# LayerNorm of the convolution branch, put inside the last four projection groups of a hybrid Conformer/gMLP layer

## Chip, cores and metric

The kernel runs on one core of one Trainium2 chip. The metric is the time of one execution on the device in microseconds (us); lower is better.

## The reference, cut to what matters

One layer over a sequence of 2048 positions with 1024 channels. A combined projection of the normalised input gives eight parts. Branch A, with which the change deals, is: GLU, a causal depthwise convolution of width 31, a LayerNorm over the channels, SiLU, a product with a SiLU gate, and a projection `w_conv_out`. Branch B is a gated mixing of positions that ends in a projection `w_sgu_out`.

```python
p = h @ w_in[l]
a = val * sigmoid(glu)
y = depthwise_causal_conv(a, conv_w) + conv_b          # width 31
y = silu(layernorm(y, ln_g, ln_b)) * silu(z)           # over the 1024 channels
y_a = y @ w_conv_out
merged = sigmoid(gA) * y_a + sigmoid(gB) * y_b
x = x + gate * (merged @ w_o[l])                       # then a final RMSNorm
```

All of it is float32. The kernel splits each operand of the large products into a high and a low part and adds three products of parts.

## The kernel before, in words

**Passes and halves.** The sequence is worked in two passes (`s` = 0 and 1) of 1024 positions, and each pass in two halves (`h`) of 512. Channels lie on the 128 partitions, in eight tiles (`j`).

**Groups.** The combined projection is made of 28 groups per pass (`quad`, L646), each a Strassen-like form of a 2 by 2 block product: seven products of 12 matmuls of 128x512 (`prod`). A group's order on TensorE is: its first product, the seventh product of the group before it (`pending`), then its second to sixth product. After the second to the sixth product an eviction follows on ScalarE or VectorE. Eight times come the three groups `glu(j)`, `uz(j)`, `spilled(j)`; the last four groups make the SiLU gate `z`, which is written to DRAM (`d_sz`) and read again later. Weight pieces are prepared four pieces ahead (`AHEAD`): a high half on ScalarE (L87) and a low half on GpSimd or VectorE (L88).

**The order of the work.** The code is traced from top to bottom, and every instruction gets a priority number in that order. The framework's planner then simulates the program and writes a fixed order of instructions for each engine: where several are ready, the one with the lowest number goes first. Each engine on the chip runs its list in that order and waits where an input is late. A background list `bg` holds small units of work; `run_bg(n)` (L319) traces the next n of them with 800 (`LATER`) added to their numbers, so that they fill gaps. It is called seven times with n = 2 in a group (six times where no `pending` is there), and with n = 4 after each product block of the two projections that follow.

**The convolution** (L693) is such background work: per tile `j` one ScalarE step and 30 VectorE steps of 128x1024 (L704), which sum in `wide()`, a pair of PSUM banks with one buffer, then `add_y` (L715), which adds the tile into `s1`. Those of the last tile run into the first of the last four groups.

**The LayerNorm** stands after the groups, on the list of the projection of branch B (`std_pairs(yb, ...)`): `mean(h)` sums `s1` over the channels with a matmul with ones (L166); `centre(h, j)` subtracts it (L835), squares (L839, L842) and adds (L843) into `rsq`; `ln_rstd(h)` makes the sums of columns with four matmuls of one column (L144), a root and a reciprocal (L137, L138), and spreads the result over the partitions (L154, L161, L852). `mean` and `ln_rstd` take PSUM banks from the six that the products use too. `conv_out(h, j)` (L854) then applies scale, SiLU and `z`, and splits the result into `ya[h][j]`. In the first pass 18 units for the token statistics of the next pass stand ahead of these on the list. `std_pairs(ya, ...)`, the projection of branch A, needs the `ya` tiles of a half as its inputs. Each of the two projections has 16 product blocks of 24 matmuls.

**Buffers.** `s1` and `rsq` share a single buffer of the tag `row`. The products and the norm share `t512` (six buffers). `yb` and `ya` come from 28 buffers `hs`, which the operands of the groups hold until the groups have used them. Loads of `z`, of the gates and of `x` for the statistics share three buffers `ld`.

Of the kernel before, what the change touches and what calls it, by code (L numbers as in the profile page):

```python
# [10 lines left out]
AF = mybir.ActivationFunctionType  # L11
ALU = mybir.AluOpType
# [4 lines left out]
D = 1024  # L17
SEQ = 2048
KT = D // P
KH = KT // 2  # L20
T = 512
S = 2 * T
NS = SEQ // S
NC = T // P
# [11 lines left out]
LATER = 800  # L36
# [4 lines left out]
def hybrid_layer(  # L41
    ctx: ExitStack, tc, x, xt, wada, wgate, vecs, rows, wst, w_in, w_v, w_a, w_b, w_o, out
):
    nc = tc.nc
# [9 lines left out]
    def bank():  # L54
        return ps.tile([P, 512], F32, tag="ps", name="bank", bufs=6)

    def wide():
        return ps.tile([P, S], F32, tag="cv", name="cv", bufs=1)

    def t512(name="t512", dtype=F32):  # L60
        return tmp.tile([P, T], dtype, tag="t512", name=name, bufs=6)
# [11 lines left out]
    def row(name):  # L73
        return tmp.tile([P, S], F32, tag="row", name=name, bufs=1)

    def load(src, name="ld"):
        t = tmp.tile([P, T], F32, tag="ld", name=name, bufs=3)
        nc.sync.dma_start(out=t, in_=src)
        return t
# [18 lines left out]
    def col(base, j):  # L98
# [4 lines left out]
    ones = const.tile([P, P], F32, name="ones")  # L103
# [3 lines left out]
        out=ident, in_=ones, pattern=[[1, P]], compare_op=ALU.is_ge, fill=0.0,  # L107
# [3 lines left out]
        out=ident, in_=ident, pattern=[[-1, P]], compare_op=ALU.is_ge, fill=0.0,  # L111
# [22 lines left out]
    def rstd_cols(src, n):  # L134

        c = sm.tile([P, 8], F32, tag="cols", name="cols")[:, :n]
        nc.scalar.activation(c, src, AF.Sqrt, bias=eps_t, scale=1.0 / D)  # L137
        nc.vector.reciprocal(out=c, in_=c)  # L138
        return c

    def col_sums(val, pt, first, n):

        for c in range(n):
            nc.tensor.matmul(  # L144
                pt[:, first + c : first + c + 1], val[:, c * P : (c + 1) * P], one,
                start=True, stop=True,
            )

    def spread(cols, pt=None):

        diag = t512("diag")
        nc.vector.tensor_tensor(  # L154
            out=diag.rearrange("p (c t) -> p c t", t=P),
            in0=ident.rearrange("p (c t) -> p c t", c=1).broadcast_to([P, NC, P]),
            in1=cols.rearrange("p (c t) -> p c t", t=1).broadcast_to([P, NC, P]),
            op=ALU.mult,
        )
        pt = bank() if pt is None else pt  # L160
        nc.tensor.matmul(pt, ones, diag, start=True, stop=True)  # L161
        return pt

    def sums(val):
        pt = bank()
        nc.tensor.matmul(pt, ones, val, start=True, stop=True)  # L166
        return pt
# [149 lines left out]
    bg = []  # L317

    def run_bg(n):  # L319
        tc.cur_priority += LATER  # L320
        for _ in range(min(n, len(bg))):
            bg.pop(0)()
        tc.cur_priority -= LATER


    def load_xn(s, h, xn):
# [135 lines left out]
    with tc.manual_schedule(engines=MANUAL):  # L462
        nc.vector.tensor_copy(out=base[:, :, 0], in_=vec[:, V_BSH : V_BSH + KT])
        nc.vector.scalar_tensor_tensor(
            out=base[:, :, 1], in0=vec[:, V_BSC : V_BSC + KT], scalar=1.0,
            in1=vec[:, V_GPRE : V_GPRE + KT], op0=ALU.add, op1=ALU.mult,
# [8 lines left out]
        for k in range(KT):  # L475
            v = xn[k][:, :T]
            if k == 0:
                nc.scalar.activation(acc, v, AF.Square)
            else:
                q = t512("q")  # L480
                nc.scalar.activation(q, v, AF.Square)
                nc.vector.tensor_tensor(out=acc, in0=acc, in1=q, op=ALU.add)
        pc = bank()
# [30 lines left out]
        for k in range(KT):  # L514
            t, v = A[0][k], xn[k][:, :T]
            nc.vector.tensor_tensor(
                out=t[:, 1], in0=v, in1=t[:, 0].bitcast(F32), op=ALU.subtract
# [17 lines left out]
            if k + 1 < KT:  # L535
                for u in range(2 * NC):
                    c, n = u // 2, u % 2
# [3 lines left out]
                for u in range(2 * NC):  # L541
                    c, n = u // 2, u % 2
# [6 lines left out]
        for u in range(2 * NC):  # L549
            c, n = u // 2, u % 2  # L550
# [6 lines left out]
            if u == 5:  # L557
                pc = bank()
# [13 lines left out]
        out=ws3, in_=ws3, pattern=[[0, KT], [1, P]], compare_op=ALU.is_ge, fill=0.0,  # L572
# [17 lines left out]
    for s in range(NS):  # L590
# [55 lines left out]
        def quad(c11, c12, c22, c21, in_psum):  # L646

            tt = nc.vector.tensor_tensor

            def snap(pt):  # L650
                t = t512("snap")
                nc.scalar.activation(t, pt, AF.Copy)  # L652
                return t

            a, d = bank(), bank()
            prod(a, [take()], A11)
            nc.scalar.activation(d, a, AF.Copy)  # L657
            run_bg(2)
            if pending:
                pending.pop()()  # L660
                run_bg(2)
            prod(a, [take()], A12, start=False)
            c11(a)
            run_bg(2)
            c = bank()
            prod(c, [take()], S1)
            p5 = snap(c)
            run_bg(2)
            prod(d, [take()], S2, start=False)
            p16 = snap(d)  # L670
            run_bg(2)
            if beside:
                beside.pop()()
            prod(c, [take()], S4, start=False)
            dst = c if in_psum else p16
            tt(out=dst, in0=c, in1=p16, op=ALU.subtract)
            c12(dst)
            run_bg(2)
            prod(d, [take()], S3, start=False)
            tt(out=p5, in0=p5, in1=d, op=ALU.subtract)  # L680
            c22(p5)
            run_bg(2)

            def end():
                prod(d, [take()], A22, start=False)
                c21(d)

            pending.append(end)

        s1 = []  # L690
        y = [None] * KT
# [90 lines left out]
        def spilled(func, d0, d1):  # L782


            def from_psum(dst):
                def fin(pt):
                    t = t512("sp")
                    nc.scalar.activation(t, pt, func)
                    nc.scalar.dma_start(out=dst, in_=t)

                return fin

            def from_sbuf(dst):
                def fin(p):
                    nc.scalar.activation(p, p, func)
                    nc.scalar.dma_start(out=dst, in_=p)

                return fin

            quad(  # L800
                from_psum(d0[0]), from_sbuf(d1[0]), from_sbuf(d1[1]), from_psum(d0[1]), False
            )

        for j in range(KT):
            glu(j)
            uz(j)
            spilled(AF.Sigmoid, d_sa[j], d_sbg[j])
        for i in range(KH):
            spilled(AF.Silu, d_sz[2 * i], d_sz[2 * i + 1])
        pending.pop()()  # L810
        run_bg(len(bg))


        yb = [[], []]
        for h in range(2):
            for j in range(KT):
                t = hs("yb")
                nc.sync.dma_start(
                    out=t.bitcast(F32).rearrange("p s c -> p (s c)"), in_=d_yb[j][h]
                )  # L820
                yb[h].append(t)

        pmu = []
        rsq = []
        ya = [[None] * KT, [None] * KT]

        def mean(h):
            pmu.append(sums(s1[0][:, h * T : (h + 1) * T]))

        def centre(h, j):  # L830
            hh = slice(h * T, (h + 1) * T)
            if not rsq:
                rsq.append(row("rsq"))
            v = y[j][:, hh]
            nc.vector.scalar_tensor_tensor(  # L835
                out=v, in0=pmu[h], scalar=-1.0 / D, in1=v, op0=ALU.mult, op1=ALU.add
            )
            if j == 0:
                nc.scalar.activation(rsq[0][:, hh], v, AF.Square)  # L839
            else:  # L840
                q = t512("q")
                nc.scalar.activation(q, v, AF.Square)  # L842
                nc.vector.tensor_tensor(  # L843
                    out=rsq[0][:, hh], in0=rsq[0][:, hh], in1=q, op=ALU.add
                )

        def ln_rstd(h):
            hh = slice(h * T, (h + 1) * T)
            pc = bank()
            col_sums(rsq[0][:, hh], pc, 0, NC)  # L850
            pr = spread(rstd_cols(pc[:, :NC], NC), pc)
            nc.scalar.activation(rsq[0][:, hh], pr, AF.Copy)  # L852

        def conv_out(h, j):  # L854
            hh = slice(h * T, (h + 1) * T)
            v = y[j][:, hh]
            z = load(d_sz[j][h], "zl")
            nc.vector.tensor_tensor(out=v, in0=v, in1=rsq[0][:, hh], op=ALU.mult)
            nc.scalar.activation(v, v, AF.Silu, bias=col(V_LNB, j), scale=col(V_LNG, j))
            nc.vector.tensor_tensor(out=v, in0=v, in1=z, op=ALU.mult)  # L860
            ya[h][j] = hs("ya")
            split(ya[h][j], v)

        if not last:
            rs_next = []
            for h in range(2):
                ss, sq = token_stats(s + 1, h)
                bg.extend(sq)
                bg.append(lambda ss=ss, h=h: rs_next.append(token_rstd(ss, f"rsn{h}")))
        for h in range(2):  # L870
            bg.append(lambda h=h: mean(h))
        for h in range(2):
            bg.extend(lambda h=h, j=j: centre(h, j) for j in range(KT))
            bg.append(lambda h=h: ln_rstd(h))
        for h in range(2):
            bg.extend(lambda h=h, j=j: conv_out(h, j) for j in range(KT))

        def std_pairs(rhs, done):

# [52 lines left out]
        if s == 0:  # L932
            for n in range(2):
# [3 lines left out]
                    out=gate[:, ns], in0=sums(acc[0][:, ns]), in1=bg_row, op=ALU.add  # L937
# [193 lines left out]
```

## Time and profile before

| | us |
|---|---|
| median of 3 runs | 1946.08 (1945.91 to 1950.67) |
| the profiled execution | 1949.32 |
| its span, first to last instruction | 1947.6 |

| engine | busy us in the span |
|---|---|
| TensorE | 1859.1 (95%) |
| VectorE | 1290.7 (66%) |
| ScalarE | 867.6 (45%) |
| GpSimd | 859.9 (44%) |

The mean granted clock of TensorE is 0.98 of 2.4 GHz. A busy share is an average over stages with different limits; matmuls overlap, so a busy TensorE is not one at its peak. What ended a wait is inferred from semaphores.

### The profile page before, as it was taken

To read this page: it belongs to the slowest core of one execution; us is meant where nothing else is said; L and a number is where in the kernel's file an instruction comes from. 1 tells how busy PE (TensorE), PEld (TensorE's weight loads), DVE (VectorE), ACT (ScalarE), POOL (GpSimd) and SP (SyncE) were. 2 spreads that over 40 slices of the span, in tenths; PEclk is the share of its full clock that TensorE was granted. 3 is DMA by queue.
4 is the path that set the end of the run, shared out by engine and by line. 5 is a ranking of instruction groups with operands and counts; after the bars stand their busy time and mean duration, and the time that the engine had idled before them with its cause. 6 is when DMAs were issued, how large, how long until landed. Compare 5 with 4: busy or idle time off the path is not lost.

```text
span 1947.6 us, 23204 instructions
## 1 busy us (share of the span) xinstructions
PE 1859.1 (95%) x8116; PEld 1517.4 (78%) x8116; DVE 1290.7 (66%) x1636; ACT 867.6 (45%) x1396; POOL 859.9 (44%) x734
## 2 busy tenths in 40 slices
PE   6798999999999998889999999999999999899998
PEld 4577888888888886668888878888888888677886
DVE  6776898888888127475851578889888861845424
ACT  4645555555546435322611455554555453532102
POOL 0035777777777710000100477777777774000000
PEclk9899999999999998889999999999999999899999
DMA  9562332222334384387886332333322246536484
GB/s 331 174 238 92 109 114 100 101 87 92 114 103 146 132 328 137 107 292 243 330 308 220 120 141 75 105 114 103 114 92 97 77 141 253 173 111 198 132 331 169
DMA packets 139015, 313.66 MB, mean 161 GB/s; under 512 B 15889, under 2 KB 16017, under 8 KB 138898
## 3 DMA queue, kind: packets, MB, share of 16 engines
q1 hardware_dynamic: 108434, 237.03, 36.2%
q0 software_dynamic: 11888, 41.43, 5.5%
q10 hardware_dynamic: 18576, 33.73, 4.6%
q8 instruction: 63, 1.03, 0.2%
q14 instruction: 54, 0.44, 0.1%
HBM read 226.66 MB, written 85.46 MB: 160 GB/s over the span
## 4 chain that ended last, share of the span: by engine, by line
PE 74%; issue 11%; DMA 7%; DVE 4%; ACT 3%; POOL 2%; SPq 0%; POOLq 0%; ACTq 0%; DVEq 0%
PE bank L297 21%; PE bank L300 21%; PE bank L303 21%; PE bank L312 3%; PE bank L313 3%; PE bank L314 3%; DMA wo<-d_wo 1%; PE bank L426 1%; DVE wa L387 1%; POOL whl L88 1%; DMA raw<-in_w_v 1%; DMA wa<-in_wada 1%; DMA xn<-in_xt 1%; DMA whl<-d_wo 1%; POOL raw L224 1%
## 5 line engine op out<-in xcount | busy, mean ns | idle before, releaser
L88 POOL TENSOR_TENSOR whl<-raw,whl 128x512 fp32r<-128x512 f32 x392 | 512.8, 1313 | 335.3 <-ACT whl L87 331.1
L704 DVE SCALAR_TENSOR_TENSOR cv<-a,vec,cv 128x1024 f32<-128x1024 f32 x464 | 596.6, 1286 | 31.6 <-ACT cv L698 21.4
L87 ACT ACTIVATE whl<-raw 128x512 fp32r<-128x512 f32 x504 | 314.3, 627 | 414.1 <-PE bank L303 214.7
L300 PE MATMUL bank<-s,whl 128*128 128x512 f32 x896 | 349.3, 390 | 1.7 <-DVE s L88 1.7
L303 PE MATMUL bank<-s,whl 128*128 128x512 f32 x896 | 349.7, 390 | 0.0
L297 PE MATMUL bank<-s,whl 128*128 128x512 f32 x896 | 349.4, 390 | 0.0
L224 POOL TENSOR_TENSOR raw<-raw 128x512 f32<-128x512 f32 x224 | 290.3, 1296 | 17.2
L297 PE MATMUL bank<-h,whl 128*128 128x512 f32 x672 | 264.0, 393 | 0.3 <-ACT bank L657 0.2
L300 PE MATMUL bank<-h,whl 128*128 128x512 f32 x672 | 261.8, 390 | 0.0
L303 PE MATMUL bank<-h,whl 128*128 128x512 f32 x672 | 261.6, 389 | 0.0
L300 PEld LDWEIGHTS bank<-s,whl 128*128 128x128 f32 x896 | 168.6, 188 | 38.0 <-DVE s L88 3.0
L297 PEld LDWEIGHTS bank<-s,whl 128*128 128x128 f32 x896 | 168.6, 188 | 34.9
L303 PEld LDWEIGHTS bank<-s,whl 128*128 128x128 f32 x896 | 168.7, 188 | 34.7
L297 PEld LDWEIGHTS bank<-h,whl 128*128 128x128 f32 x672 | 126.1, 188 | 32.5 <-DVE snap L680 5.3
L303 PEld LDWEIGHTS bank<-h,whl 128*128 128x128 f32 x672 | 126.1, 188 | 26.5
L300 PEld LDWEIGHTS bank<-h,whl 128*128 128x128 f32 x672 | 126.2, 188 | 25.6
L88 DVE TENSOR_TENSOR whl<-raw,whl 128x512 fp32r<-128x512 f32 x112 | 75.9, 688 | 96.9 <-ACT whl L87 91.8
L892 POOL DMA_DIRECT2D mb<-gl x32 | 17.3, 541 | 275.0 <-DVE gl L891 264.3
L297 PE MATMUL bank<-ya,whl 128*128 128x512 f32 x256 | 102.6, 401 | 13.8 <-ACT ya L87 10.6
L652 ACT ACTIVATE snap<-bank 128x512 f32<-128x512 f32 x112 | 66.5, 598 | 98.0 <-PE bank L303 98.0
L297 PE MATMUL bank<-yb,whl 128*128 128x512 f32 x256 | 105.4, 412 | 4.2 <-DVE gl L891 3.5
L300 PE MATMUL bank<-ya,whl 128*128 128x512 f32 x256 | 102.6, 401 | 1.4 <-DVE ya L88 1.4
(214 smaller groups left out, 2867.3 us busy)
## 6 DMA issues: line engine op xcount, KB each, us to landing
raw<-in_w_in SPq DMA_DIRECT2D x224, 256.0 KB, 3.0
yb<-yb SPq DMA_DIRECT2D x32, 512.0 KB, 7.6
whl<-d_wo SPq DMA_DIRECT2D x32, 512.0 KB, 4.6
whl<-d_wv SPq DMA_DIRECT2D x32, 512.0 KB, 4.3
xn<-in_xt SPq DMA_DIRECT2D x32, 256.0 KB, 5.4
wa<-in_wada SPq DMA_DIRECT2D x16, 512.0 KB, 6.5
raw<-in_w_v SPq DMA_DIRECT2D x32, 256.0 KB, 4.8
d_wv<-whl POOLq DMA_DIRECT2D x16, 512.0 KB, 6.5
```

What stands on the lines that cost most here:

```text
L87: nc.scalar.activation(hi, val, AF.Copy)
L88: eng.tensor_tensor(out=lo, in0=val, in1=hi.bitcast(F32), op=ALU.subtract)
L224: eng.tensor_tensor(out=dst, in0=dst, in1=src, op=ALU.add)
L297: nc.tensor.matmul(pt, wh, h[:, 0], start=start and k == 0, stop=False, skip_group_check=True)
L300: nc.tensor.matmul(pt, wh, h[:, 1], start=False, stop=False, skip_group_check=True)
L303: nc.tensor.matmul(pt, wl, h[:, 0], start=False, stop=k == last, skip_group_check=True)
L312: nc.tensor.matmul(pt, xh, w[:, 0], start=kt == 0, stop=False)
L313: nc.tensor.matmul(pt, xh, w[:, 1], start=False, stop=False)
L314: nc.tensor.matmul(pt, xl, w[:, 0], start=False, stop=kt == KT - 1)
L387: nc.vector.tensor_tensor_reduce(out=wa[i], in0=wa[i], in1=cbc, scale=col(V_GPRE, k) if i else 1.0, scalar=0.0, op0=ALU.mult, op1=ALU.add, ...
L652: nc.scalar.activation(t, pt, AF.Copy)
L704: nc.vector.scalar_tensor_tensor(out=dst, in0=a[:, k : k + S], scalar=col(V_CW, j * TAPS + k), in1=cv[0], op0=ALU.mult, op1=ALU.add,)
```

## The change

The LayerNorm's units are put on the background list ahead of the last four groups, behind what is left of the last tile's convolution, and so they are traced inside these groups. Empty units (`pause`) stand between them. Four kinds of unit are `urgent`: they are traced with the 800 taken off again, at normal priority: `mean` (now one unit for both halves), `ln_cols` (column sums, root, reciprocal) and `ln_spread` (spreading) of each half. The sums, columns and spread values lie in one `wide()` tile, the convolution's PSUM pair, bank 0 for half 0 and bank 1 for half 1, and not in banks of the products' six. The flush `run_bg(len(bg))` behind the groups goes. On the list of the projection of branch B, `conv_out` now stands ahead of the token statistics.

```diff
+    def urgent(f):
+        def run():
+            tc.cur_priority -= LATER
+            f()
+            tc.cur_priority += LATER
+        return run
+    def pause(n):
+        bg.extend([lambda: None] * n)
...
+        def mean():
+            stat.append(wide())
+            for h in range(2):
+                nc.tensor.matmul(
+                    stat[0][:, half(h)], ones, s1[0][:, half(h)], start=True, stop=True
+                )
+        def centre(h, j):
...
+            nc.vector.scalar_tensor_tensor(
+                out=v, in0=stat[0][:, half(h)], scalar=-1.0 / D, in1=v,
...
+        def ln_cols(h):
+            col_sums(rsq[0][:, half(h)], stat[0], h * T, NC)
+            rcols[h] = rstd_cols(stat[0][:, h * T : h * T + NC], NC)
+        def ln_spread(h):
+            pr = spread(rcols[h], stat[0][:, half(h)])
+            nc.scalar.activation(rsq[0][:, half(h)], pr, AF.Copy)
...
+        pause(3)
+        bg.append(urgent(mean))
+        pause(1)
+        for h in range(2):
+            bg.extend(lambda h=h, j=j: centre(h, j) for j in range(KT))
+            if h:
+                bg.append(urgent(lambda: ln_spread(0)))
+            else:
+                pause(2)
+            bg.append(urgent(lambda h=h: ln_cols(h)))
+        pause(4)
+        bg.append(urgent(lambda: ln_spread(1)))
         for i in range(KH):
             spilled(AF.Silu, d_sz[2 * i], d_sz[2 * i + 1])
         pending.pop()()
-        run_bg(len(bg))
...
+        for h in range(2):
+            bg.extend(lambda h=h, j=j: conv_out(h, j) for j in range(KT))
         if not last:
 ...
-        for h in range(2):
-            bg.append(lambda h=h: mean(h))
-        for h in range(2):
-            bg.extend(lambda h=h, j=j: centre(h, j) for j in range(KT))
-            bg.append(lambda h=h: ln_rstd(h))
-        for h in range(2):
-            bg.extend(lambda h=h, j=j: conv_out(h, j) for j in range(KT))
```

## Rows read from the trace of the kernel before

**Rows 1.** The page: busy us, share of the span and instructions by engine.

```profile
PE 1859.1 (95%) x8116; PEld 1517.4 (78%) x8116; DVE 1290.7 (66%) x1636; ACT 867.6 (45%) x1396; POOL 859.9 (44%) x734
```

**Rows 2.** Windows over both projections, passes 0 and 1; PEclk is the granted clock.

```profile
695.50:803.70 108.20, 98.48 (x414) 79.48 (x413) 54.64 (x89) 39.83 (x72) 7.05 (x13) 0.94 0.57 190
803.70:917.40 113.70, 97.09 (x393) 76.81 (x392) 68.26 (x114) 33.57 (x51) 3.75 (x7) 0.91 0.67 221
1647.90:1763.30 115.40, 102.62 (x421) 81.70 (x421) 69.84 (x113) 48.97 (x75) 6.49 (x12) 0.93 0.50 170
1763.30:1850.40 87.10, 87.10 (x386) 72.10 (x386) 40.52 (x61) 16.65 (x27) 2.16 (x4) 1.00 0.49 155
```

**Rows 3.** Timeline of TensorE, pass 0; in brackets the idle time before, and its releaser.

```profile
725.60 1.88 PE L166 MATMUL bank<-s,ones 128*128 128x512 f32 x4
...
745.99 0.48 PE L144 MATMUL bank<-one,rsq 128*128 128x1 f32 x2 [2.15 <-DVE rsq L843]
...
758.85 0.72 PE L144 MATMUL bank<-one,rsq 128*128 128x1 f32 x6
760.96 1.10 PE L161 MATMUL bank<-diag,ones 128*128 128x512 f32 x2 [1.38 <-ACT q L842]
768.24 0.58 PE L144 MATMUL bank<-one,rsq 128*128 128x1 f32 x2 [6.19 <-DVE rsq L843]
...
822.83 0.80 PE L297 MATMUL bank<-ya,whl 128*128 128x512 f32 x1 [5.08 <-ACT ya L87]
...
842.17 0.80 PE L297 MATMUL bank<-ya,whl 128*128 128x512 f32 x1 [5.51 <-ACT ya L87]
...
872.09 0.53 PE L297 MATMUL bank<-ya,whl 128*128 128x512 f32 x1 [2.02 <-ACT whl L87]
```

**Rows 4.** Windows of the wait before 768.24 and of the time behind it.

```profile
762.50:768.20 5.70, 0.00 (x0) 0.00 (x0) 5.60 (x11) 5.67 (x9) 0.00 (x0) 0.56 0.18 47
768.20:773.00 4.80, 4.76 (x12) 3.89 (x13) 4.25 (x7) 3.47 (x6) 0.00 (x0) 0.50 0.39 113
```

**Rows 5.** Timeline of TensorE, pass 1.

```profile
1689.08 0.59 PE L144 MATMUL bank<-one,rsq 128*128 128x1 f32 x2 [5.82 <-DVE rsq L843]
...
1756.15 0.55 PE L297 MATMUL bank<-yb,whl 128*128 128x512 f32 x1 [2.15 <-DVE gl L891]
```

**Rows 6.** Windows of the second and third of the last four groups (third in pass 1).

```profile
637.80:657.40 19.60, 19.38 (x85) 15.69 (x84) 1.79 (x4) 12.59 (x23) 15.31 (x13) 1.00 0.39 139
657.40:676.50 19.10, 19.10 (x86) 15.79 (x85) 1.38 (x2) 8.00 (x14) 14.46 (x12) 1.00 0.33 112
1610.00:1629.00 19.00, 19.00 (x86) 15.73 (x85) 1.38 (x2) 8.01 (x14) 14.04 (x12) 1.00 0.31 111
```

**Rows 7.** Timeline of TensorE: the second group's first matmul, passes 0 and 1.

```profile
637.83 0.39 PE L297 MATMUL bank<-h,whl 128*128 128x512 f32 x1
...
1590.83 0.39 PE L297 MATMUL bank<-h,whl 128*128 128x512 f32 x1
```

**Rows 8.** Timeline of VectorE: the last `add_y`, and an eviction, passes 0 and 1.

```profile
634.47 1.69 DVE L715 TENSOR_TENSOR s<-s,a 128x1024 f32<-128x1024 f32 x1
...
1588.36 0.69 DVE L676 TENSOR_TENSOR snap<-bank,snap 128x512 f32<-128x512 f32 x1 [0.72 <-PE bank L303]
1588.97 1.22 DVE L715 TENSOR_TENSOR s<-s,a 128x1024 f32<-128x1024 f32 x1
```

**Rows 9.** Groups of instructions from 690 to 850 us: busy us, mean ns, idle before.

```profile
L835 DVE SCALAR_TENSOR_TENSOR a<-bank,a 128x512 f32<-128x512 f32 x16 | 10.5, 679 | 0.0
L843 DVE TENSOR_TENSOR rsq<-rsq,q 128x512 f32<-128x512 f32 x14 | 9.6, 683 | 0.9 <-ACT q L842 0.7
L842 ACT ACTIVATE q<-a 128x512 f32<-128x512 f32 x14 | 7.9, 620 | 1.3 <-DVE a L835 1.2
L137 ACT ACT_TABLE_LOAD x1 | 1.3, 1283 | 0.0
```

**Rows 10.** Waits of TensorE on ScalarE in the last four groups, 618 to 696 us.

```profile
PE bank L297 <- ACT bank L657: 0.2, 1, 0.2
```

More of the change, by code (lines that the diff above doesn't have):

```diff
@@ L802, in spilled, with half @@
             )
+        stat = []
+        rsq = []
+        rcols = [None, None]
+        ya = [[None] * KT, [None] * KT]
+        def half(h):
+            return slice(h * T, (h + 1) * T)
+        def mean():
[5 more added lines that the diff above has]
+        def centre(h, j):
+            if not rsq:
+                rsq.append(row("rsq"))
+            v = y[j][:, half(h)]
+            nc.vector.scalar_tensor_tensor(
+                out=v, in0=stat[0][:, half(h)], scalar=-1.0 / D, in1=v,
+                op0=ALU.mult, op1=ALU.add,
+            )
+            if j == 0:
+                nc.scalar.activation(rsq[0][:, half(h)], v, AF.Square)
+            else:
+                q = t512("q")
+                nc.scalar.activation(q, v, AF.Square)
+                nc.vector.tensor_tensor(
+                    out=rsq[0][:, half(h)], in0=rsq[0][:, half(h)], in1=q, op=ALU.add
+                )
+        def ln_cols(h):
[4 more added lines that the diff above has]
+            nc.scalar.activation(rsq[0][:, half(h)], pr, AF.Copy)
         for j in range(KT):
@@ L807, in hybrid_layer @@
             spilled(AF.Sigmoid, d_sa[j], d_sbg[j])
+        pause(3)
[5 more added lines that the diff above has]
+                bg.append(urgent(lambda: ln_spread(0)))
+            else:
+                pause(2)
+            bg.append(urgent(lambda h=h: ln_cols(h)))
+        pause(4)
+        bg.append(urgent(lambda: ln_spread(1)))
         for i in range(KH):
@@ L821, in hybrid_layer @@
                 yb[h].append(t)
[L823 to L852, printed above, removed]
         def conv_out(h, j):
```

## The prediction

> **What bounds the kernel now.** I read the page first. TensorE is busy for 95% of the span and no other engine for more than 66% [rows 1], so time is won only where TensorE waits, or runs at its lower clock, and is lost only where it is made to. The view that finds such places is the table of windows, laid over the stages around the change. The two projections behind the groups are equal in work: 16 blocks of 24 matmuls each. One of the four, branch A's in pass 1, runs without a gap at a granted clock of 1.00 and takes 87.1 us for its 384 matmuls, 0.227 us for one; the other three take 108.2, 113.7 and 115.4 us at 0.91 to 0.94 [rows 2]. The groups themselves show no such loss: 19.0 to 19.6 us for 84 matmuls at a clock of 1.00 [rows 6].
>
> The timeline of TensorE says what is lost in the slow three. In pass 0 it waits 2.15 us for the squares of half 0 (L843) at a column sum, 1.38 us at the spreading, 6.19 us for the squares of half 1; then, in branch A's projection, 5.08 and 5.51 us for `ya` tiles that are not written yet [rows 3]. In pass 1 the same column sum waits 5.82 us, and a block waits 2.15 us for an eviction behind the burst of `conv_out` [rows 5]. So it is the norm that comes too late: its chain stands in the middle of a stage that needs its result at the end. Behind a long wait the clock is lower too: after the 6.19 us wait 12 matmuls take 4.8 us at a granted clock of 0.50, that is 1.2 GHz [rows 4], where 12 at 0.227 take 2.7; a wait of this size costs another 2.1 us.
>
> **What the change removes.** The loss is the two projections' time, less twice 87.1, less what is real work. In pass 0: 108.2 + 113.7 - 174.2 = 47.7 us. Real work in it is the groups' last product, 12 matmuls, 2.7 us, and the norm's own matmuls: 1.88 for the means, 1.10 for each spreading, about 1.0 for each half's eight column sums (six take 0.72) [rows 3], together 6.1. That leaves 38.9 us. In pass 1: 115.4 + 87.1 - 174.2 = 28.3, less the same 8.8: 19.5. Together **58.4 us** can be won; the 6.1 us a pass are not saved, they move into the groups.
>
> One piece of it is not the norm's: at 872.09 a block waits 2.02 us for a weight piece [rows 3], with slow matmuls behind it, for which I put 2.1 [rows 4]. I let **4.1 us** of it stay (bounds 0 and 4.1; an earlier norm moves the loads ahead of that piece, and I can't see which way).
>
> **What the change adds to the groups.** VectorE gets 16 subtractions and 14 additions (10.5 + 9.6 us a pass) and ScalarE 16 squares, 14 of them 7.9 us [rows 9], and two roots with a table load of 1.28 us on either side: at most 5.1. The last conv step is over when the second group begins; from then on VectorE is busy for 1.8 and 1.4 us of the second and third group, ScalarE for 12.6 and 8.0 [rows 6]. So VectorE has some 35 us free for 20 us of work. ScalarE has 18 free for about 9 + 5 + 1.2 for the copies, which is close, but the fourth group is there as well. The evictions behind which this work queues, or which queue behind it, free PSUM banks that are needed a group later, and the weight pieces are four products (10.9 us) ahead; this cover is what makes the edit free on both engines. The one short place is the copy L657, which the group's second product needs one product later: it made TensorE wait 0.2 us, once, in pass 0 [rows 10]. With squares ahead of it I allow 0.3 us in each of three groups and two passes: **2 us** (bounds 0 and 13, which is six times 2.15, the next larger wait [rows 3]).
>
> The urgent matmuls can make TensorE wait, since everything behind them stands in its list. The mean needs the last `add_y`. It is traced between a group's fourth and fifth product, but the planner lets it go only when, by its own clock, `add_y` is over. In pass 0 the group ends at 637.83 [rows 7], so the fourth product ends at 632.4 and the fifth at 635.1; `add_y` runs from 634.47 to 636.16 [rows 8]. The planner put `add_y` ahead of the eviction that waits for the fifth product, so by its clock it began before 635.1; placed right behind the fifth product the mean waits 1.1 us, and behind the fourth 3.8. In pass 1 the eviction stands ahead of `add_y`, though VectorE on the chip was free 0.72 us before it could run [rows 8], so by the planner's clock VectorE is later there than on the chip, and the mean should find its input ready. I take **1.1 us** for both passes (bounds 0 and 3.8 + 4.8; 1590.83 less 24 matmuls is 1585.4, `add_y` ends at 1590.19). The sums of columns: half 0 needs 15 VectorE steps of 0.66 us (10.5 for 16 [rows 9]) behind the mean, some 10 us, so it is ready near 648 to 650; the unit is traced behind the second group's third product, at 637.83 + 4 x 2.72 + 1.9 = 650.6. Half 1 needs 15 more steps, near 659, and is traced in the third group behind its first two products, near 664. That is 0 to 2 us of slack, and 5 us. For the four of them I take 0.5 us each, **2 us** (bounds 0 and 6.19 + 2.1 each). The spreadings have ten us and more of slack, and the pair of banks is free: the last convolution step has left it before `add_y`, and the next convolution is hundreds of us away.
>
> Nothing is added to the DMA queues; the `z` loads go ahead of the statistics' loads of `x` in SP's queue, and GpSimd's queue keeps its order. `conv_out` needs 48 VectorE steps, 32 us at 0.66, in a stage in which VectorE is now busy for 54.6 us with the centring's 20 taken out. `ya` needs `hs` buffers: 28 less 16 for `yb`, so twelve tiles at once and the last four near the end of branch B's projection, a half's two blocks (10.9 us) before they are needed.
>
> **The sum.** 1949.3 of the profiled execution - 58.4 + 4.1 + 2 + 1.1 + 2 = 1900.1. The profiled execution lies 3.2 us above the median of the runs, so I expect a median of **1897 us**.
>
> **The rivals.**
> (1) *The norm is early, but `ya` is not.* `conv_out` waits for `z` loads, which share three buffers with the gates, and for `hs` buffers; the two waits in front of branch A's projection in pass 0 stay. They cost 5.08 + 5.51 and twice 2.1 [rows 3, 4], 15 us: 1912. For it: in pass 0 all of the list was late. Against it: in pass 1, with 18 units fewer ahead, that projection has no wait at all [rows 2].
> (2) *The waits move into the groups.* If the planner's clock for VectorE runs ahead of the chip's, each urgent step stands in front of TensorE's list too early. What that is the trace shows: at 768.24 the column sum held TensorE for 6.19 us [rows 3], and the slow stretch behind it cost 2.1 [rows 4]. With 3.8 and 4.8 us at the means and 2.1 behind each, and 8.3 at each of four column sums, that is 46 us in place of the 3.1 that I took: 1940 at the worst, near 1920 if half of it comes. Against it: the groups' order, from the same planner, leaves 0.2 us of waits. The Trainium skill, TensorE: Matmul & The Clock Gate, "Architectural detail" (engine queue depths), says that matmuls stay in program order and only weight loads are pulled ahead. By that rule a late urgent step holds all matmuls behind it, which would give this rival's time; the trace agrees, with the 6.19 us wait at 768.24.
> (3) *Slower.* ScalarE becomes the bound of the groups: its list is fixed, squares wait in it for VectorE, and the high halves of the weights behind them come late. TensorE then runs at ScalarE's pace. It decides if the last three groups become longer by 26 us a pass, 84 us where they take 58, which would undo the 52 us that the sum gives; every us beyond it makes the kernel slower, at 90 us some 12 us: 1958. Against it: ScalarE's 12.6 + 8 + 8 and 16 us added are 45 us in 58.
> (4) *Nothing happens*: the planner puts the urgent steps where they were. 1946. They would need an input that it thinks late by 60 us; nothing shows that.
>
> **How the numbers follow.** Forecast (1884 to 1907): 0.62. Rival 1: 0.16, rival 2: 0.15, rival 3: 0.05, rival 4: 0.02. The low end is the whole 58.4 us won, 1888, and a few us for loads that come earlier in the stage behind; the high end takes in rival 1 and the lower half of rival 2, up to 1926. Within 0.3%, about what a measurement here can tell from no change, is 1940.2 to 1951.9: rival 4 and the tail of rival 2, 0.03. Slower is rival 3, 0.05; faster is the rest, 0.92.
>
> **What would show it.** Right: the windows of both projections near 87 to 92 us at a clock of 0.97 or more in both passes; L144 and L161 at 650 to 675 us with waits under 1 us; no wait on `ya`; the last three groups at 19 to 21 us. Wrong: waits on L843 or L715 in the groups and a clock below 0.9 there (rival 2), waits on ScalarE's `ya` near 790 to 810 us (rival 1), the groups stretched with waits on L87 or L657 (rival 3). The forecast fails most easily by the slack of the four column sums, and by the weights of branch A's projection in pass 0, when its loads are pressed into 87 us.

## The result, and the profile after

The changed kernel takes 1917.13 us (median of 4 runs, 1916.35 to 1918.98) where the kernel before, timed beside it, takes 1946.37 (1945.91 to 1950.67): a ratio of 0.9845, 95% interval 0.983 to 0.9861. It is faster by about 29 us. The forecast was 1897 us, with a range of 1884 to 1926: direction and range hold, and the gain is 0.6 of the one forecast. The time lies outside the band of the forecast itself (1884 to 1907), in the part of the range that was left to the rivals.

The profiled execution took 1916.63 us, its span is 1914.7. The page's first part, after; the columns are those of [rows 1]:

```profile
PE 1846.7 (96%) x8116; PEld 1507.4 (79%) x8116; DVE 1332.7 (70%) x1636; ACT 862.5 (45%) x1394; POOL 873.8 (46%) x734
```

VectorE has as many instructions as before and is busy for 42 us longer. Something made its instructions slower; that is the clue to most of what follows.

Windows of the kernel after, columns as in [rows 2]. The first and fourth are the last three groups of passes 0 and 1; behind each stand the two projections, branch B's and then branch A's:

```profile
639.88:710.80 70.92, 64.97 (x274) 51.45 (x273) 56.82 (x62) 49.49 (x82) 40.98 (x27) 0.95 0.46 164
710.80:802.80 92.00, 91.12 (x398) 73.95 (x397) 37.53 (x66) 33.55 (x70) 7.04 (x13) 1.00 0.79 272
802.80:899.60 96.80, 89.58 (x386) 73.06 (x385) 55.23 (x86) 19.05 (x31) 3.76 (x7) 0.96 0.70 233
1575.52:1642.40 66.88, 61.92 (x274) 49.46 (x273) 55.63 (x63) 49.70 (x82) 41.54 (x27) 1.00 0.48 175
1642.40:1732.30 89.90, 89.90 (x397) 74.25 (x396) 40.25 (x61) 21.44 (x35) 8.12 (x15) 1.00 0.67 231
1732.30:1819.40 87.10, 87.10 (x386) 72.10 (x385) 39.65 (x58) 17.09 (x27) 0.54 (x1) 1.00 0.42 133
```

The projections took 108.2 + 113.7 and 115.4 + 87.1 us [rows 2]; now 188.8 and 177.0. Pass 1 has nothing left to win (176.9 was forecast). Pass 0 keeps 11.9 us over that. The three groups, 57.7 and 57.1 us before (from the second group's first matmul [rows 7] to branch B's), are now 70.9 and 66.9.

TensorE's timeline after, pass 0, to set beside [rows 3], with some matmuls behind two of the waits:

```profile
636.77 1.88 PE L829 MATMUL cv<-s,ones 128*128 128x512 f32 x4
...
653.03 1.05 PE L144 MATMUL cv<-one,rsq 128*128 128x1 f32 x8 [1.41 <-DVE rsq L846]
...
654.91 0.63 PE L297 MATMUL bank<-s,whl 128*128 128x512 f32 x1
655.33 0.63 PE L300 MATMUL bank<-s,whl 128*128 128x512 f32 x1
...
672.53 1.12 PE L161 MATMUL cv<-diag,ones 128*128 128x512 f32 x2 [1.51 <-DVE diag L154]
...
685.35 2.08 PE L161 MATMUL cv<-diag,ones 128*128 128x512 f32 x2 [3.03 <-DVE diag L154]
...
687.65 0.63 PE L297 MATMUL bank<-s,whl 128*128 128x512 f32 x1
...
818.19 0.80 PE L303 MATMUL bank<-ya,whl 128*128 128x512 f32 x1 [6.64 <-DVE whl L88]
```

And pass 1, to set beside [rows 5]:

```profile
1605.38 1.12 PE L161 MATMUL cv<-diag,ones 128*128 128x512 f32 x2 [1.72 <-DVE diag L154]
...
1618.20 1.13 PE L161 MATMUL cv<-diag,ones 128*128 128x512 f32 x2 [3.00 <-DVE diag L154]
```

The waits on `ya` are gone, the mean (L829) waits for nothing, and three of four column sums (L144) wait for nothing. All four spreadings (L161) wait, and a weight piece in branch A's projection comes 6.64 us late. Groups of VectorE's and GpSimd's instructions from 636 to 712 us, to set beside [rows 9]:

```profile
L88 POOL TENSOR_TENSOR whl<-raw,whl 128x512 fp32r<-128x512 f32 x19 | 27.9, 1470 | 22.9 <-ACT whl L87 22.9
L892 DVE TENSOR_TENSOR a<-a,rsq 128x512 f32<-128x512 f32 x16 | 21.0, 1361 | 2.8 <-ACT rsq L856 2.8
...
L846 DVE TENSOR_TENSOR rsq<-rsq,q 128x512 f32<-128x512 f32 x14 | 15.4, 1100 | 4.7 <-ACT q L845 4.3
...
L837 DVE SCALAR_TENSOR_TENSOR a<-cv,a 128x512 f32<-128x512 f32 x16 | 10.1, 677 | 1.6 <-PE cv L829 1.6
...
L154 DVE TENSOR_TENSOR diag<-ident,cols 128x512 f32<-128x512 f32 x2 | 2.4, 1214 | 0.0
```

The addition (L846) that took 683 ns [rows 9] takes 1100, the first product of the convolution's output (L892) 1361, the two diagonals (L154) 1214 in the mean. The subtraction L837 stays at 677. The first three read two tiles of SBUF; L837 reads one, and the PSUM pair. What is new around them is GpSimd, 41 us busy in the first of the windows above and 8.7 in the 160 us in which [rows 9] were taken.

VectorE's timeline, and GpSimd's of the same stretch behind it, say how this reaches TensorE:

```profile
668.10 2.71 DVE L846 TENSOR_TENSOR rsq<-rsq,q 128x512 f32<-128x512 f32 x2 [0.71 <-ACT q L845]
670.73 1.75 DVE L154 TENSOR_TENSOR diag<-ident,cols 128x512 f32<-128x512 f32 x1
...
674.33 6.38 DVE L892 TENSOR_TENSOR a<-a,rsq 128x512 f32<-128x512 f32 x5 [1.25 <-ACT rsq L856]
680.64 0.17 DVE L138 RECIPROCAL cols<-cols 128x4 f32<-128x4 f32 x1
680.73 3.96 DVE L892 TENSOR_TENSOR a<-a,rsq 128x512 f32<-128x512 f32 x3
684.61 0.68 DVE L154 TENSOR_TENSOR diag<-ident,cols 128x512 f32<-128x512 f32 x1
...
688.09 0.69 DVE L892 TENSOR_TENSOR a<-a,rsq 128x512 f32<-128x512 f32 x1 [1.59 <-ACT rsq L856]
```

```profile
675.38 1.40 POOL L88 TENSOR_TENSOR whl<-raw,whl 128x512 fp32r<-128x512 f32 x1 [3.44 <-ACT whl L87]
676.85 3.31 POOL L224 TENSOR_TENSOR raw<-raw 128x512 f32<-128x512 f32 x2
680.13 1.74 POOL L88 TENSOR_TENSOR whl<-raw,whl 128x512 fp32r<-128x512 f32 x1
682.15 1.39 POOL L88 TENSOR_TENSOR whl<-raw,whl 128x512 fp32r<-128x512 f32 x1 [0.28 <-ACT whl L87]
689.77 1.68 POOL L88 TENSOR_TENSOR whl<-raw,whl 128x512 fp32r<-128x512 f32 x1 [6.23 <-ACT whl L87]
```

The column sums of half 1 end at 675.4, and their reciprocal (L138) stands in VectorE's list behind five products, the diagonal behind three more. At 0.68 us these eight would take 5.4 us; they take 10.3. TensorE waits 3.03 us of it.

The single instructions show whose doing it is. From 636 to 712 us VectorE runs 36 instructions of 128x512 with both inputs in SBUF (L846, L892, L894, L154). The 13 that start while GpSimd rests, such as those at 684.61 and 688.09, take 0.67 to 0.69 us. The 23 that start while an instruction of GpSimd runs take 0.84 to 1.79 us, and each ends 0.55 us behind the end of that instruction.

### The profile page after: what moved, and what is told of

The parts are those of the page before. It is cut to its first block, busy times and chain, and to the rows that moved or that the text cites. A ratio compares the mean times of both kernels' runs of the same rounds, so it can differ in the third digit from the quotient of the medians.

```text
span 1914.7 us, 23225 instructions
## 1 busy us (share of the span) xinstructions
PE 1846.7 (96%) x8116; PEld 1507.4 (79%) x8116; DVE 1332.7 (70%) x1636; ACT 862.5 (45%) x1394; POOL 873.8 (46%) x734
## 4 chain that ended last, share of the span: by engine, by line
PE 75%; issue 9%; DVE 6%; DMA 5%; ACT 3%; POOL 2%; SPq 0%; ACTq 0%; POOLq 0%; DVEq 0%
PE bank L297 21%; PE bank L303 21%; PE bank L300 21%; PE bank L312 3%; PE bank L313 3%; PE bank L314 3%; DVE a L892 1%; DMA raw<-in_wgate 1%; DVE wa L400 1%; PE bank L439 1%; DMA wa<-in_wada 1%; POOL whl L88 1%; DMA xn<-in_xt 1%; DMA whl<-d_wo 1%; ACT whl L87 1%
## 5 line engine op out<-in xcount | busy, mean ns | idle before, releaser
L88 POOL TENSOR_TENSOR whl<-raw,whl 128x512 fp32r<-128x512 f32 x392 | 520.9, 1333 | 348.5 <-ACT whl L87 344.0
L224 POOL TENSOR_TENSOR raw<-raw 128x512 f32<-128x512 f32 x224 | 295.8, 1321 | 17.2
L303 PE MATMUL bank<-ya,whl 128*128 128x512 f32 x256 | 100.6, 393 | 6.7 <-DVE whl L88 6.6
L297 PE MATMUL bank<-ya,whl 128*128 128x512 f32 x256 | 100.4, 392 | 0.5 <-ACT whl L87 0.5
L297 PE MATMUL bank<-yb,whl 128*128 128x512 f32 x256 | 99.8, 390 | 0.9 <-ACT whl L87 0.9
```

The source lines that it names most:

```text
L88: eng.tensor_tensor(out=lo, in0=val, in1=hi.bitcast(F32), op=ALU.subtract)
L224: eng.tensor_tensor(out=dst, in0=dst, in1=src, op=ALU.add)
L297: nc.tensor.matmul(pt, wh, h[:, 0], start=start and k == 0, stop=False, skip_group_check=True)
L303: nc.tensor.matmul(pt, wl, h[:, 0], start=False, stop=k == last, skip_group_check=True)
```

## The experiments

Each ratio is to the kernel before, timed beside it on the same chip. The experiments ran on four chips (e1 to e4, e5 to e8, e9 to e11, e12) and `after` apart from them, so versions are compared by ratios; that a version has the same ratio on every chip no run shows.

| run | median us | ratio, 95% interval |
|---|---|---|
| after | 1917.13 | 0.9845, 0.983 to 0.9861 |
| e1_both_copies_late | 1914.43 | 0.9813, 0.9799 to 0.9828 |
| e2_product_from_psum | 1914.61 | 0.9814, 0.9798 to 0.983 |
| e3_not_urgent | 1926.2 | 0.9868, 0.9851 to 0.9886 |
| e4_statistics_behind | 1955.37 | 1.0028, 1.0017 to 1.0039 |
| e5_wa_low_on_gpsimd | 1925.94 | 0.9864, 0.9837 to 0.9892 |
| e6_groups_low_on_vector | 1915.24 | 0.9818, 0.9787 to 0.985 |
| e7_sums_in_banks | 1920.81 | 0.9845, 0.9819 to 0.9872 |
| e8_combined | 1927.13 | 0.9875, 0.9841 to 0.9908 |
| e9_gate_later | 1912.59 | 0.9806, 0.9789 to 0.9822 |
| e10_psum_gate_later | 1910.27 | 0.9791, 0.977 to 0.9812 |
| e11_psum_groups_on_vector | 1913.19 | 0.9806, 0.9791 to 0.9822 |
| e12_statistics_spaced | 1911.64 | 0.9807, 0.9781 to 0.9833 |

**What slows VectorE in the groups.** The theory: its operations with two operands in SBUF wait for GpSimd. The rivals: VectorE's list is simply too full, or its order alone is at fault.

e6 takes GpSimd out of the last four groups:

```diff
-            eng = nc.gpsimd
+            eng = nc.vector if q >= NQ - 4 else nc.gpsimd
```

> In the last four groups GpSimd does nothing: the additions and low halves of the weights are made on VectorE. Theory A (VectorE's operations with two SBUF operands are slow because GpSimd works at the same time): L846 falls from 0.98 to 1.10 us to about 0.69, L892 from 1.36 to about 0.69, though VectorE has some 30 us of work more in 76; the waits at the spreadings fall from 1.5 and 3.0 us to under 1, ratio 0.979 to 0.984. Theory B (they are slow for the number of operations in VectorE's list, or for ScalarE beside it): L846 and L892 stay above 0.95 us and the waits grow, ratio above 0.986.

The same groups of instructions in e6, from 636 to 712 us:

```profile
L837 DVE SCALAR_TENSOR_TENSOR a<-cv,a 128x512 f32<-128x512 f32 x16 | 10.5, 681 | 0.9 <-PE cv L829 0.9
L892 DVE TENSOR_TENSOR a<-a,rsq 128x512 f32<-128x512 f32 x16 | 10.0, 681 | 0.0
L846 DVE TENSOR_TENSOR rsq<-rsq,q 128x512 f32<-128x512 f32 x14 | 9.6, 684 | 0.2
...
L154 DVE TENSOR_TENSOR diag<-ident,cols 128x512 f32<-128x512 f32 x2 | 1.4, 682 | 0.0
```

All are back at 0.68 us although VectorE now does the weights' additions and low halves too (61.4 us busy from 640 to 712, 57.7 in the kernel after). So GpSimd beside it made these instructions slow, and not the length of the list. No L144 or L161 waits, in either pass. That may have a second reason: the planner's order is another one, with the mean at 649.4 us where it was at 636.8. Branch B's projection begins at 705.5 us where it began at 710.8. In pass 1 the groups win nothing: from the end of pass 0's projections to branch B's projection it is 743.1 us, as in the kernel after (742.8), because the new order has waits on evictions and a weight piece (1.27, 1.21, 0.78 and 1.52 us) in place of the 4.7 us at the spreadings. In the whole, the interval overlaps that of the kernel after.

e2 leaves GpSimd alone and takes away one SBUF operand: the first product reads the spread values where the spreading wrote them, in PSUM, and their copy goes.

```diff
-            pr = spread(rcols[h], stat[0][:, half(h)])
-            nc.scalar.activation(rsq[0][:, half(h)], pr, AF.Copy)
+            spread(rcols[h], stat[0][:, half(h)])
...
-            nc.vector.tensor_tensor(out=v, in0=v, in1=rsq[0][:, hh], op=ALU.mult)
+            nc.vector.tensor_tensor(out=v, in0=v, in1=stat[0][:, hh], op=ALU.mult)
```

> conv_out's first product reads the spread value from the PSUM pair instead of a copy in SBUF; its count, size and engine are the same. Theory A with GpSimd as the cause (two SBUF operands are slow while GpSimd works): that product falls from 1.36 us in the groups to 0.68, the second spreading's wait falls from 3.0 us to about 0.5, GpSimd's operations get faster by 5% or so in the last groups, and the time is 1908 to 1913. If VectorE is slow in the groups for another reason (its instruction rate, waits on ScalarE), the product stays above 1.1 us and the time at 1915 to 1919.

The product's group in e2, from 636 to 712 us:

```profile
L891 DVE TENSOR_TENSOR a<-a,cv 128x512 f32<-128x512 f32 x16 | 9.9, 676 | 6.6 <-PE cv L161 6.6
```

That product (L891 here) takes 676 ns in place of 1361, and the second spreading waits no more; the first one, whose operations ahead still read two SBUF tiles, waits 1.48 us as before. Branch B's projection begins at 705.1. But the two projections of pass 0 together then take 193 us where they took 188.8: three quarters of the 5.7 us that the groups won are given back before 898 us. Branch B's projection of pass 0 takes 95.1 to 98.5 us in every run in which it begins before 707 us (e1, e2, e6, e7, e10, e11, e12), and 92.0 in the kernel after, where it begins at 710.8.

e1 keeps the copies and makes both behind the second spreading, so that no product of the output can stand ahead of that spreading's diagonal:

```diff
+            if h:
+                for i in range(2):
+                    nc.scalar.activation(rsq[0][:, half(i)], stat[0][:, half(i)], AF.Copy)
```

> Both halves' spread values are copied to SBUF only after the second spreading, so no product of conv_out can stand in VectorE's list ahead of the second diagonal. Theory A (VectorE's list is late because of the products with two SBUF operands in front of the diagonal, eight at 1.28 us): the second spreading's wait of 3.0 us in each pass falls under 1 us, its slow matmuls go too, and the time falls by 6 to 10 us against the changed kernel, to 1907 to 1911. Theory B (the waits come from the urgent priority as such, which puts the step in front of TensorE's list before its input is there, whatever stands ahead on VectorE): the wait stays at 2 to 3 us and the time stays at 1915 to 1919.

The second spreading's wait goes here too, and the ratio is that of e2. So those 3 us go either way, by a product that GpSimd doesn't hold up or by an order with no product ahead; this pair of runs alone would not have told why the instructions were slow; e6 and the single instructions above do.

e11 is e2 and e6 together.

> The first product from PSUM and, in the last four groups, the weight additions and low halves on VectorE, so that GpSimd computes nothing there. If all that slowed the groups was VectorE beside GpSimd, the second edit alone (ratio 0.9818) has removed it, and the first adds no more than the two copies on ScalarE: 1913 to 1916 us, ratio 0.981 to 0.982. If VectorE's list was also simply full in the groups, the two add up: 1908 to 1911 us, ratio 0.978 to 0.980. The mean of the squares' additions is 0.68 to 0.69 us in either case.

Within the intervals the ratio is that of either alone, as it should be where the two edits cure one fault.

**What the parts of the change are worth.** e3 takes the normal priority away (`run` only calls `f`):

> The TensorE steps of the norm keep the list's 800 on their numbers; place on the list, PSUM pair and order of conv_out are those of the changed kernel. If the priority is what brings the gain, the sums run only where TensorE is idle in the planner's clock, in branch B's projection again, and the time is 1935 to 1950 with waits on L846 there. If the place on the list alone does it, the time is 1908 to 1918, with no waits of L144 or L161 in the groups.

Both bounds missed: most of the gain comes without it. The planner then puts the mean at 655.6 us in place of 636.8 and the first spreading at 693.3, where it waits 4.47 us; the second comes at 714.0, when branch B's projection has begun (708.4). Earlier units give the gain; the priority adds some 4 us, with intervals that overlap.

e7 takes two of the products' six banks for the sums, instead of the convolution's pair:

> The sums lie in two banks of the products' six, held from the mean to the second spreading, instead of the convolution's pair. If the pair is a needed part of the gain, four banks are left for groups that use three each, evictions are waited for (L297 on L665, L689 or L693) and the last groups become longer by 5 us or more a pass: ratio 0.989 or more. If four banks are enough, the ratio is 0.983 to 0.986 as with the pair.

The ratio is that of the kernel after: the pair earns nothing that these runs can show.

e4 makes one part of the change in the kernel before: the statistics of the next pass go behind `conv_out` on the list.

> The kernel before with one edit: the 18 units of token statistics stand behind the norm and conv_out on the list. If pass 0 lost more than pass 1 because of these units, its two projections fall from 221.9 us to about the 202.5 of pass 1, the waits on ya go, and the time is 1925 to 1930; pass 1 is unchanged. If the statistics were hidden anyway, the time stays at 1946.

Slower, by 0.3%, which neither expectation had. The first spreading comes at 731 us where it came at 761 [rows 3], but the loads of `x` now fall on the end of branch B's projection, and share the three `ld` buffers with the gates that an eviction (L891) needs. Timeline of TensorE in e4:

```profile
807.36 0.80 PE L297 MATMUL bank<-yb,whl 128*128 128x512 f32 x1 [4.01 <-DVE gl L891]
...
822.03 0.80 PE L297 MATMUL bank<-ya,whl 128*128 128x512 f32 x1 [6.35 <-DVE gl L891]
...
832.21 0.47 PE L297 MATMUL bank<-ya,whl 128*128 128x512 f32 x1 [2.33 <-DVE gl L891]
```

By itself, in the kernel before, the reordering is a cost. What it is worth once the norm has left that stage no run shows.

**What holds pass 0's projections.** VectorE's timeline of the kernel after, ahead of the 6.64 us wait:

```profile
816.05 0.49 DVE L936 TENSOR_SCALAR acc<-raw,vec 128x512 f32<-128x512 f32 x1 [9.89 <-DMA raw<-in_wgate]
816.79 0.75 DVE L940 SCALAR_TENSOR_TENSOR acc<-raw,vec,acc 128x512 f32<-128x512 f32 x1 [0.25 <-DMA raw<-in_wgate]
817.45 0.68 DVE L88 TENSOR_TENSOR whl<-raw,whl 128x512 fp32r<-128x512 f32 x1
```

A step of the layer's gate vector, background work, waits 9.89 us for its load; the low half of a weight piece stands behind it. e5 takes that low half off VectorE's list:

```diff
-            split(w, part(mat, q, kh, c))
+            split(w, part(mat, q, kh, c), nc.gpsimd if mat is w_a else nc.vector)
```

> The low halves of branch A's weight pieces are made on GpSimd, which is idle in the projections, instead of VectorE. If branch A's projection in pass 0 loses its 6.64 us because the piece's low half stands in VectorE's list behind a gate step that waits for its load (theory A), the wait and its slow matmuls go, some 8 us, and the ratio to the kernel before is 0.980 to 0.982 where the changed kernel has 0.9845. If the load of the piece itself or the stage's DMA traffic is what is late (theory B), the wait moves to GpSimd's list or to the load and the ratio stays at 0.983 to 0.986.

Not better. The wait moved to a later piece and grew to 10.93 us. Two lines of e5's view of the tile `raw`, 800 to 845 us (instructions, then shortest, median and longest in ns, first and last start):

```profile
L174 SPq DMA_DIRECT2D raw<-in_wgate x15: 328/369/1278, 810.6 to 831.4; - x15
...
L174 SPq DMA_DIRECT2D raw<-in_w_a x8: 328/333/430, 831.9 to 845.0; - x8
```

15 of the gate's 16 loads are issued on SP's queue ahead of the next weight pieces, and both take the same eight buffers. The same view of the kernel after has that order too:

```profile
L174 SPq DMA_DIRECT2D raw<-in_wgate x15: 327/328/582, 809.2 to 829.3; - x15
...
L174 SPq DMA_DIRECT2D raw<-in_w_a x8: 327/328/430, 829.8 to 841.1; - x8
```

There TensorE, held up by the 6.64 us, comes to these pieces later and waits 0.50 us for one of them. So the engine of the low half was not the fault; that it is the place of the gate's steps, e9 tests below. e8 joins e2, e5 and three more pauses, and fails in the same place (a wait of 11.00 us), worse than either of its expectations:

```diff
+                pause(1)
                 bg.append(urgent(lambda: ln_spread(0)))
             else:
-                pause(2)
+                pause(4)
```

> Three edits together: conv_out's first product reads the spread value from PSUM, branch A's weights get their low halves on GpSimd, and two empty units more stand ahead of the first column sums and one ahead of the first spreading. If the waits seen in the changed kernel are independent (theory A), the waits of 1.4, 1.5 to 1.7 and 3.0 us in the groups and the 6.6 us in branch A's projection all go, and the ratio is 0.975 to 0.979. If pass 0 is bound by its loads (theory B), what is won in the groups of pass 0 comes back as waits in its projections, as in the two runs before, and the ratio is 0.980 to 0.982.

In pass 0 the first spreading also waits longer, 3.27 us. e9 moves the gate's steps themselves:

```diff
+            pause(24)
             bg.extend(lambda r=r, n=n: gate_step(r, n) for r in range(KT) for n in range(2))
```

> The changed kernel with 24 empty units ahead of the gate's 16 steps, so that their loads and their accumulations on VectorE come six products later in branch A's projection of pass 0. Theory (the 6.64 us wait at 818 is VectorE's list: a gate step waits 9.89 us for its load and stands ahead of the low half of a weight piece): the wait falls under 2 us, the half-clock stretch behind it goes, the sums over the gate (899.6) come 6 to 8 us sooner, 1909 to 1912 us, ratio 0.980 to 0.982. Rival (the transfers themselves are full at 805 to 816, with a DMA share of 0.91 to 1.01, and some load is late whatever stands where): the wait moves to the weight piece's own load or to an output's gate, 1915 to 1919 us, ratio 0.983 to 0.986.

TensorE's longest wait in branch A's projection of pass 0 in e9:

```profile
827.59 0.50 PE L297 MATMUL bank<-ya,whl 128*128 128x512 f32 x1 [1.29 <-ACT whl L87]
```

This is what the theory said. The largest wait of TensorE in that projection is 1.29 us, and the sums over the gate start at 894.0 us where they started at 899.6; 1.4 us of this was there when branch B's projection began. e10 adds e2's edit:

> The first product of the convolution's output read from PSUM, its copy dropped (as in the earlier run, ratio 0.9814), and the gate's steps 24 units later. If the two faults are separate (VectorE's slow operations in the groups, a late load on VectorE's list in the projection) their gains add up: 1906 to 1910 us, ratio 0.977 to 0.979. If what the groups gain is taken back by the transfers in pass 0 whatever the order of the list, as with the product alone: 1913 to 1915 us, ratio 0.981.

0.9791 is the lowest ratio here, by its middle value most of the two gains together. Its interval lies clear of the kernel after's, as do those of e1, e9 and e11; but it overlaps those of e9, e11 and e12, so that the gains add up is not shown beyond the noise. In the trace part is still given back: branch B's projection takes 97 us, and a wait of 3.09 us stands in branch A's. ScalarE's timeline in e10 shows one cause:

```profile
778.14 0.63 ACT L353 ACTIVATE xs<-xs 128x512 f32<-128x512 f32 x1 [1.56 <-DMA xs<-in_x]
...
780.32 0.63 ACT L353 ACTIVATE xs<-xs 128x512 f32<-128x512 f32 x1 [1.46 <-DVE gl L919]
...
780.94 0.61 ACT L87 ACTIVATE whl<-raw 128x512 fp32r<-128x512 f32 x1
```

Squares for the next pass's statistics wait for their loads, and the high half of a weight piece stands behind them; TensorE waits 2.69 us for it. With `conv_out` done sooner these come sooner, among the weights' loads; that their waits come from this is not shown. e12 puts an empty unit ahead of each:

```diff
-                bg.extend(sq)
+                for f in sq:
+                    pause(1)
+                    bg.append(f)
```

> The version with the product from PSUM and the gate's steps later (ratio 0.9791), with one empty unit ahead of each of the 16 statistics units, so that they come over twice as many products of branch B's projection in pass 0. Theory (that projection loses what the groups gained because squares on ScalarE wait for their loads and stand ahead of weight pieces: 1.31 us at 758.70, 2.69 us at 781.61, matmuls of 0.63 us behind it): those waits fall under 1 us, branch B's projection goes from 97 to 92 us, the sums over the gate come from 896.4 to about 892, 1904 to 1908 us, ratio 0.976 to 0.978. Rival (loads are late because the transfers are full in pass 0, share 0.75 to 1.03): as before it, 1909 to 1914 us, ratio 0.979 to 0.981; or worse, if the spaced units run into the gate's loads, over 0.981.

Not settled. In its trace the sums over the gate start at 892.2 us, as the theory has it, and that execution took 1908.05 us; the four runs reach to 1915.31, the ratio is no better than e10's, and a wait of 2.60 us on ScalarE stays at 783.78. How much of pass 0 is order and how much is the transfers themselves, which are 0.79 busy in branch B's window above, stays open.

## Why the prediction came out so

The forecast was 20.1 us too low, and its range holds only by what it takes in of the rivals. 3.7 us of it are the profiled executions: that of before lies 3.2 us above its median, that of after 0.5 below. The rest are terms of the sum:

| term | forecast us | measured us |
|---|---|---|
| projections of pass 0 | 181.0 | 188.8 |
| projections of pass 1 | 176.9 | 177.0 |
| the norm in the groups, beyond its 6.1 us of matmuls a pass | 5.1 | 14.8 |
| between the passes' stages, and after them | 0 | -1.2 |

The third row is, in pass 0, 2.05 us until the second group's first matmul (637.83 to 639.88) and the 13.2 by which three groups grew; in pass 1 the 1.88 of the mean and 9.8; less 6.1 each. The last is 0.7 more from the end of branch A's projection to the next pass's groups, and 1.9 less behind the last projection.

**The loss to be won was read rightly.** 58.4 us in the four projections less what stays: pass 1 came out to 0.1 us, and no block waits for `ya`. Rival 1 is out.

**The step that failed: "the spreadings have ten us and more of slack", at no cost.** They wait 1.51, 3.03, 1.72 and 3.00 us, 9.3 together, and behind the 3.03 us the matmuls lose another 1.6 us at lower clock (from the spreading to the fifth matmul behind it 3.45 us, at the same place of pass 1 1.89). The four column sums, which the prediction feared most, wait 1.41 us in all, with slow matmuls behind it (nine starts 0.43 us apart where 0.227 is full pace, 1.6 us); the means wait for nothing (2 us had been allowed for the sums, 1.1 for the means), and of the copies' 2 us nothing is seen. The slack was counted with VectorE at 0.66 us a step, from rows of a stretch where GpSimd rests, and a stretch in which GpSimd works was filled with it. And the list was longer than counted: the prediction had `conv_out` in the projections, but all 16 of its first products in a pass run in the groups, 21.0 us, eight of them ahead of the second diagonal. The second spreading's wait needs both, slow products and their place: e2 makes them short, e1 puts them behind the diagonal, and each edit alone takes the wait away. For the first spreading and the column sum no run parts the length of VectorE's operations from their order. The mechanism is rival 2's: an urgent step stands too early in TensorE's list, since VectorE on the chip is later than in the plan; that follows from the order and the waits, the plan's own times are not on record. Only its size is smaller: 9.7 us above the sum, not the 23 of that rival's half. In e6, where VectorE keeps 0.68 us, no matmul of the norm waits for VectorE, though in another order. Rival 3's "52 us that the sum gives" is 49.2 in the sum itself (1949.3 less 1900.1).

The row that should have warned stood in the prediction's own list. `add_y` took 1.69 us in pass 0 and 1.22 in pass 1 [rows 8]: the same instruction with both operands in SBUF, and the prediction used its end without asking why its length differed. In e6, with GpSimd at rest, it takes 1.22 in pass 0 too. The Trainium skill, SBUF — State Buffer, "Who interferes with whom" and "Summary: rules for kernel authors", has the rule: a VectorE instruction with two SBUF inputs contends with a GpSimd instruction that reads SBUF, the one that starts later waits for the whole of the other, and one with at most one SBUF input does not contend. The trace agrees on who is slowed (1361, 1214 and 1100 ns against 677) and on the wait (all 23 end 0.55 us behind GpSimd's instruction); what it adds is the price in such a mix, in the mean some 0.4 to 0.7 us an operation, and that GpSimd pays as well (1470 ns for its low halves here, 1313 over the kernel before).

**The term that was seen and mis-sized: the weights of branch A in pass 0.** 4.1 us were left for it; 11.9 us over full pace stay in the two projections. 6.64 us is the one long wait, with 1.4 us of half-clock matmuls behind it, and e9 shows that it hangs on where the gate's loads stand. The rest, 2.1 us in branch B's projection and some 1.7 in branch A's, is small waits on weight pieces of ScalarE (0.50, 0.38 and 0.50 us) and slower starts around the waits.

**Rivals 3 and 4** did not happen. The groups stretched by 13.2 and 9.8 us of the 26 a pass that rival 3 needed, and in none of them does TensorE wait for ScalarE.

## What to carry to other kernels

Before work is put under the cover of another stage, take its durations from rows in which the same other engines work; an operation whose length differs between two places of one trace is the hint to look for. Where the move brings VectorE beside GpSimd, leave one operand in PSUM if it already is there. And an in-order list is only as early as the late load that stands ahead of it: where background steps stood ahead of a weight piece, taking the piece to another engine moved the wait (e5), and moving the steps took it away (e9). Part of what is won ahead of such a stage can be given back in it (e2, e10).

## What was not expected of the hardware

A wait of TensorE has no fixed price in clock. In the kernel after, waits of 1.41 and 3.03 us in pass 0 are followed by matmuls of 0.63 us (a granted clock of 0.66 from 652.9 to 657.8 us, 0.50 from 685.3 to 687.0), and the pair of 685.35 takes 2.08 us; in pass 1 waits of 1.72 and 3.00 us are followed by pairs of 1.12 and 1.13 us, and that whole window keeps a granted clock of 1.00. And beside a working GpSimd a single operand's place halves a VectorE instruction: 676 ns with the second operand in PSUM, 1361 with both in SBUF, on the same data in the same stretch.
